# A hybrid decoder step: probabilities times cached values, with the cached rows as the stationary operand in plain float32

## The chip, the cores and the metric

The kernel runs on one core of one Trainium2 chip. The metric is the device time of one execution in microseconds (us). It was run three times before the change: 1616.27 us is the median, 1614.43 and 1624.24 the ends. A profiled execution gives the trace that all rows below come from. PE is the matrix engine (TensorE), PEld its weight loads, DVE the vector engine, ACT the scalar engine, POOL the GpSimd engine, SP the engine that issues the DMAs. The profile gives PE's granted clock as a share of full speed; its two levels are 0.5 (1.2 GHz) and 1.0 (2.4 GHz).

## The reference

One layer of a decoder runs over a prompt of 1024 tokens and over 8 sampled sequences of 8 new tokens. The layer's input projection feeds an attention group (8 heads of 64, three dilated windows whose weights are merged) and a state-space group; their outputs are normalised and go through an output projection and a gated feed-forward network. The change concerns the attention of the sampled tokens alone, which reads 2048 cached rows of K and V for each sequence:

```python
def _branch_sample(q, k_all, v_all, window, dil):
    n = window // dil
    idx = lbuf + jnp.arange(t)[:, None] - dil * jnp.arange(n + 1)[None, :]
    ...
    kg = k_all[:, idx]
    vg = v_all[:, idx].astype(F32)
    scores = jnp.einsum('bthe,btkhe->bhtk', q, kg, preferred_element_type=F32) * (HEAD_DIM ** -0.5)
    ...
    out = jnp.einsum('bhtk,btkhe->bthe', p / den, vg)
```

The change is in how the last line is computed: for each sequence b and head h, the sum over cached rows of a probability (8 new tokens) times a row of V (64 numbers).

## The kernel before, in words

The program is one instruction stream for each engine; a planner sets the order of instructions by the timeline that it reckons, within what the code's generators (`merge`, with paces) hand it. It has these stages: the input projection (`phase_a`, with the sampled tokens' scores, `sample_scores`), then `phase_b`, then the output projection and the feed-forward network (`phase_e`), which takes more than half of the time.

`phase_b` has two halves. In the first, the state-space recurrence (`ssm_main`), the prompt's attention (`prompt_attn`) and the softmax of the first four sampled sequences run side by side. In the second, which this text calls **the value stage**, three streams run side by side: the state-space gate (`ssm_gate`, tiles mixS, w, sg), the values of the sampled tokens (`sample_values`) and the rest of the prompt's attention. Of that attention these names appear in rows: KH, KL and QS are keys and queries (scores, into a bank pmm), P the probabilities, PT their transposes (from a bank ptr), VS the values (into the bank ppo).

The numbers of most products are float32 split in two parts of the type float32r, a rounded "hi" and a remainder "lo" (`split`: an ACT copy that rounds, then a DVE or POOL subtraction), since a float32r product goes through PE in one pass; a plain float32 product appears in the trace as two matmul records with a weight load each.

`sample_values` takes 10 units of 128 cached rows for each of 8 sequences, 80 units in all. For a unit, `vload` (SP, tile vr, six buffers, five units ahead) brings 128 rows of 512 numbers (8 heads of 64). `vsplit` writes vs: hi on ACT, lo on DVE or POOL (POOL for even units). `mult` issues two matmuls: the stationary operand is PX, the probabilities of 8 heads and 8 tokens as 64 columns of hi and 64 of lo, and vs moves past it, 512 columns of hi and then of lo, so every head's probabilities meet every head's values. After the tenth unit, vn (the new rows, 64 partitions) is added with PN. The bank then holds 64 times 512 numbers of which the blocks with equal heads are wanted: `gather1` masks them with hsel and adds over heads on DVE, `gather2` turns them with a matmul by csel and two ACT copies write mixA. `soft1` to `soft3` make the probabilities of the later sequences on the way; `soft3` splits them into PX and PN.

Of the kernel before, what the change touches and what calls it, by code (L numbers as in the profile page):

```python
# [10 lines left out]
F32 = mybir.dt.float32  # L11
F32R = mybir.dt.float32r
I32 = mybir.dt.int32
AF = mybir.ActivationFunctionType
OP = mybir.AluOpType
AX = mybir.AxisListType
# [15 lines left out]
FPOOL, PPOOL, VPOOL, HSP = ((3,), (1, 3, 5), (1, 3, 5), (1, 3, 5)), ((0, 1),), (0, 2, 4, 6, 8), (1, 3, 5, 7)  # L32
XPOOL = (3, 4, 5, 6, 7, 8)
CLAG, CS, X1, LG, VG, LA, TLAG, NLAG = 1, 2, 5, 3, 4, 3, 3, 1
PB, VB, VSB, KKB, PTB, TAB, TCB, HSB, UB, CSB, WSB, HB = 10, 6, 4, 2, 2, 3, 2, 3, 2, 3, 5, 5
# [7 lines left out]
def raw(ap):  # L43
    return ap.bitcast(F32)


class K:
# [701 lines left out]
    def sample_values(self, sp):  # L749
        nc, I = self.nc, self.I  # L750
        V = nc.vector
        S = self.S
        cv = I["cache_attn_v"][0].rearrange("b p h e -> b p (h e)")
        hsel = sp.tile([128, 8], F32, name="hsel")
        sel = sp.tile([128, 68], F32, name="sel")
        csel = sp.tile([128, 64], F32, name="csel")
        self.load(hsel, I["c_hsel"])
        self.load(sel, I["c_sel"])
        self.load(csel, I["c_csel"])
        vn = sp.tile([64, 2, 512], F32R, name="vn")  # L760
        vnr = sp.tile([128, 1152], F32, tag="pv", name="vnr", bufs=1)[:64, 0:512]
        self.load(vnr, self.O[7].rearrange("o b t h e -> (o b t) (h e)"))
        self.split(vn[:, 0], vn[:, 1], vnr)
        PX, PN, mx = {}, {}, {}


        def soft1(g):
            sl = sp.tile([128, 1152], F32, tag="pv", name="sl", bufs=1)[:, 0:NKEY]
            for a in range(2):
                self.load(sl[64 * a:64 * a + 64], I["c_slnc"][2 * g + a].unsqueeze(0).to_broadcast((8, 8, NKEY)))  # L770
            mx[g] = sp.tile([128, 2], F32, tag="mx", name="mx", bufs=2)
            V.tensor_tensor_reduce(out=S[:, g], in0=S[:, g], in1=sl, scale=-1.0, scalar=3e38, op0=OP.add, op1=OP.min, accum_out=mx[g][:, 0:1])
            nc.scalar.activation(S[:, g], S[:, g], AF.Exp, bias=mx[g][:, 0:1], scale=-1.0, accum_out=mx[g][:, 1:2])

        def soft2(g):
            V.reciprocal(mx[g][:, 1:2], mx[g][:, 1:2])
            V.tensor_scalar(S[:, g], S[:, g], mx[g][:, 1:2], None, op0=OP.mult)

        def soft3(g):
            PX[g] = sp.tile([128, 2, 10, 2, 64], F32R, tag="PX", name="PX", bufs=2)
            PN[g] = sp.tile([64, 2, 2, 64], F32R, tag="PN", name="PN", bufs=2)
            Z = sp.tile([128, 1152], F32, tag="pv", name="Z", bufs=1)
            V.tensor_tensor(Z[:, 0:768].rearrange("p (a t) -> p a t", t=8), S[:, g, 0:96].unsqueeze(2).to_broadcast((128, 96, 8)),
                            sel[:, 0:8].unsqueeze(1).to_broadcast((128, 96, 8)), op=OP.mult)
            V.tensor_tensor(Z[:, 768:1152].rearrange("p (a t) -> p a t", t=4), S[:, g, 96:192].unsqueeze(2).to_broadcast((128, 96, 4)),
                            sel[:, 8:12].unsqueeze(1).to_broadcast((128, 96, 4)), op=OP.mult)
            for j0, n in ((0, 4), (4, 4), (8, 2)):
                p = self.bank("sd")  # L790
                for j in range(n):
                    src = Z[:, 128 * (j0 + j):128 * (j0 + j) + 128] if j0 + j < 9 else S[:, g, 192:320]
                    self.tr(p[:, 128 * j:128 * j + 128], src)
                if n == 2:
                    self.tr(p[:64, 256:384], S[:, g, 320:384])
                    self.split(PN[g][:, :, 0], PN[g][:, :, 1], p[:64, 256:384].rearrange("p (b c) -> p b c", b=2))
                for a in range(2):
                    pa = p[:, 0:128 * n].rearrange("p (j b c) -> p b j c", j=n, b=2)[:, a]
                    d = PX[g][:, a, j0:j0 + n]
                    self.split(d[:, :, 0], d[:, :, 1], pa)  # L800


        vr, vs, po, rb = {}, {}, {}, {}
        NU = 10

        def vload(i):
            if i >= 8 * NU:
                return
            b, u = divmod(i, NU)
            vr[i] = self.sv.tile([128, 512], F32, tag="vr", name="vr", bufs=VB)  # L810
            if u < 6:
                self.load(vr[i], cv[b, 256 * u:256 * u + 256].rearrange("(a r) f -> a r f", r=16)[:, 0:8])
            else:
                self.load(vr[i], cv[b, 768 + 128 * u:896 + 128 * u])

        def vsplit(i):
            b, u = divmod(i, NU)
            s = vs[i] = self.sv.tile([128, 2, 512], F32R, tag="vs", name="vs", bufs=VSB)
            nc.scalar.activation(s[:, 0], vr[i], AF.Copy)  # L819
            eng = nc.gpsimd if u in VPOOL else V  # L820
            eng.tensor_tensor(out=s[:, 1], in0=vr[i], in1=raw(s[:, 0]), op=OP.subtract)  # L821

        def mult(i):
            b, u = divmod(i, NU)
            if u == 0:
                po[b] = self.bank("sd")
            p, s = po[b], vs[i]
            x = PX[b // 2][:, b % 2, u].rearrange("p a c -> p (a c)")
            for hl in range(2):
                self.mm1(p, x, s[:, hl], start=(u == 0 and hl == 0), stop=False)  # L830
            if u == NU - 1:
                for hl in range(2):
                    self.mm1(p, PN[b // 2][:, b % 2].rearrange("p a c -> p (a c)"), vn[:, hl], False, hl == 1)

        def gather1(b):
            pv = sp.tile([128, 1152], F32, tag="pv", name="pv", bufs=1)[:, 0:512].rearrange("p (h e) -> p h e", e=64)
            V.tensor_tensor(pv, po[b].rearrange("p (h e) -> p h e", e=64), hsel.unsqueeze(2).to_broadcast((128, 8, 64)), op=OP.mult)
            rb[b] = sp.tile([128, 2, 64], F32, tag="rb", name="rb", bufs=1)
            V.tensor_reduce(rb[b][:, 0], pv.rearrange("p h e -> p e h"), axis=AX.X, op=OP.add)
            V.tensor_copy(rb[b][:, 1], rb[b][:, 0])  # L840

        def gather2(b):
            pa = self.bank("sd")
            self.mm1(pa[:, 0:64], rb[b].rearrange("p a e -> p (a e)"), csel)
            pav = pa[:, 0:64].rearrange("p (f a t) -> p f a t", f=4, a=2)
            cs = slice(1024 + 8 * b, 1032 + 8 * b)
            nc.scalar.activation(self.mixA[0:64, :, cs], pav[0:64, :, 0], AF.Copy)
            nc.scalar.activation(self.mixA[64:128, :, cs], pav[64:128, :, 1], AF.Copy)
        for g in range(2):
            soft1(g)  # L850
            yield 1.0
            soft2(g)
            yield 1.0
            soft3(g)
            yield 1.0
        yield None
        for i in range(VB - 1):
            vload(i)
        for i in range(8 * NU + 3):
            vload(i + VB - 1)  # L860
            if i < 8 * NU:
                vsplit(i)
            if 2 <= i < 8 * NU + 2:
                mult(i - 2)
            b, u = divmod(i, NU)
            if b < 7:

                if b % 2 == 1 and u in (1, 4, 7) and b > 1:
                    (soft1, soft2, soft3)[(1, 4, 7).index(u)](b // 2 + 1)
            if i >= NU + 2 and u == 2:  # L870
                gather1(b - 1)
            if i >= NU + 4 and u == 4:
                gather2(b - 1)
            yield 0.45
        gather2(7)


    def ssm_main(self, sp):
# [1033 lines left out]
def consts():  # L1912
    d = {"c_ident": np.eye(128, dtype=np.float32)}
# [5 lines left out]
    r = np.arange(128)[:, None]  # L1919
# [4 lines left out]
    n, m = np.arange(128)[:, None], np.arange(128)[None, :]  # L1924
# [4 lines left out]
    t = np.arange(8)[:, None]  # L1929
# [4 lines left out]
    for b in range(8):  # L1934
        new[b, :, b, :] = lnc(t - np.arange(8)[None, :])
    d["c_slnc"] = np.concatenate([np.broadcast_to(far, (8, 8, 96)), np.broadcast_to(mid, (8, 8, 96)), np.broadcast_to(near, (8, 8, 128)), new.reshape(8, 8, 64)], axis=2)

    r = np.arange(128)
    d["c_hsel"] = (r[:, None] // 8 % 8 == np.arange(8)[None, :]).astype(np.float32)
    d["c_csel"] = (r[:, None] % 64 == np.arange(64)[None, :]).astype(np.float32)  # L1940

    d["c_sel"] = np.concatenate([r[:, None] % 8 == np.arange(8), r[:, None] % 4 == np.arange(4),
                                 r[:, None] // 8 == np.arange(16), r[:, None] // 4 == np.arange(32), (r[:, None] + 4) % 8 == np.arange(8)], axis=1).astype(np.float32)
# [27 lines left out]
```

## Time and the profile before

| | |
|---|---|
| Median of 3 runs | 1616.27 us |
| Profiled execution | 1614.53 us, of which span 1612.8 us (first to last instruction) |
| Granted clock of PE over the span | 0.923 |
| Busy share of the span: PE, PEld, DVE, ACT, POOL | 91%, 84%, 74%, 45%, 54% |
| The first matmul on vs starts, the last rows on vs | 495.0 us, 659.0 us from the span's start |

A group's mean time of a PE instruction is its latency, and matmuls overlap. What one costs PE is read from the start of one row of the timeline to the start of the next, divided by the number of matmuls in it.

### The profile page before, as it was taken

The page shows a single profiled execution, that of the slowest core. Times are in us where ns is not written, and L with a number is a line of the kernel's source. Part 1 is how long each engine was busy: PE and PEld are TensorE (multiplying, and loading weights), DVE is VectorE, ACT ScalarE, POOL GpSimd, SP SyncE. Part 2 cuts the span into 40 slices and gives each one's busy share as a digit, 9 for nine tenths or more (in the row PEclk, how much of TensorE's full clock was granted, in tenths as well). Part 3 has the DMA queues.
Part 4 walks back from the last instruction along what each step waited for, and adds up shares of the span by engine and source line. Part 5 has one row for each costly group of instructions (what it writes and reads, how often), then busy time and mean ns, then how long its engine had stood idle before and what let it go on. Part 6 is the DMA issues. An engine that isn't in the chain of part 4 may idle for free.

```text
span 1612.8 us, 27931 instructions
## 1 busy us (share of the span) xinstructions
PE 1466.1 (91%) x9909; PEld 1362.1 (84%) x9909; DVE 1193.3 (74%) x2310; ACT 720.3 (45%) x1831; POOL 877.8 (54%) x807
## 2 busy tenths in 40 slices
PE   6988779788899999899887999999999979988896
PEld 5988769776777777689887999999999979978896
DVE  6887589938866787777989555555555598789785
ACT  6232334434456767665443333333333354454343
POOL 3065354407734545545568655555553386578772
PEclk9998879866878999789998999999999999999998
DMA  8445698689746873534322222333332383474654
GB/s 217 149 159 180 202 262 242 197 198 223 203 129 178 214 195 98 157 95 130 96 88 83 91 94 92 99 102 101 102 102 70 109 296 111 149 285 137 187 163 122
DMA packets 212953, 246.20 MB, mean 153 GB/s; under 512 B 26798, under 2 KB 164878, under 8 KB 212814
## 3 DMA queue, kind: packets, MB, share of 16 engines
q1 hardware_dynamic: 212814, 244.43, 51.3%
q8 instruction: 78, 1.28, 0.3%
q14 instruction: 61, 0.50, 0.1%
HBM read 184.43 MB, written 59.95 MB: 152 GB/s over the span
## 4 chain that ended last, share of the span: by engine, by line
PE 62%; DVE 18%; DMA 9%; issue 5%; POOL 3%; ACT 2%; SPq 1%; DVEq 0%; POOLq 0%; ACTq 0%
PE pmm L72 14%; PE pmm L70 14%; PE pmm L71 14%; PE psd L75 7%; PE pmm L75 4%; DVE ws L65 3%; PE ppo L75 3%; PE ptr L79 2%; DMA kk<-in_cache_attn_k_dram 1%; DVE hT L1540 1%; DVE hn L65 1%; DMA kf<-in_cache_attn_k_dram 1%; SPq L82 1%; DMA hs<-dH 1%; PE psd L79 1%
## 5 line engine op out<-in xcount | busy, mean ns | idle before, releaser
L70 PE MATMUL pmm<-hn,ws 128*128 128x272 f32 x1232 | 359.0, 291 | 10.2 <-DVE s L1694 6.4
L72 PE MATMUL pmm<-hn,ws 128*128 128x272 f32 x1232 | 357.2, 291 | 3.4 <-DVE ws L65 3.4
L71 PE MATMUL pmm<-hn,ws 128*128 128x272 f32 x1232 | 357.4, 290 | 2.1 <-DVE hn L65 2.1
L65 DVE TENSOR_TENSOR ws<-wr,ws 128x512 fp32r<-128x512 f32 (+2 forms) x240 | 254.9, 1071 | 32.1 <-ACT ws L64 31.5
L70 PEld LDWEIGHTS pmm<-hn,ws 128*128 128x128 f32 x1232 | 233.9, 190 | 11.1 <-issue 7.7
L71 PEld LDWEIGHTS pmm<-hn,ws 128*128 128x128 f32 x1232 | 234.1, 190 | 2.8 <-DVE hn L65 2.7
L72 PEld LDWEIGHTS pmm<-hn,ws 128*128 128x128 f32 x1232 | 232.9, 189 | 4.0 <-DVE ws L65 3.9
L64 ACT ACTIVATE ws<-wr 128x512 fp32r<-128x512 f32 (+2 forms) x240 | 152.5, 642 | 176.5 <-PE pmm L72 169.1
L65 DVE TENSOR_TENSOR ws<-st,ws 128x512 fp32r<-128x512 f32 (+1 forms) x136 | 132.5, 978 | 81.3 <-ACT ws L64 80.6
L64 ACT ACTIVATE ws<-st 128x512 fp32r<-128x512 f32 (+1 forms) x136 | 83.6, 616 | 135.7 <-PE pmm L72 101.5
L72 PE MATMUL pmm<-hs,ws 128*128 128x272 f32 x448 | 133.6, 299 | 8.5 <-DVE ws L65 7.8
L70 PE MATMUL pmm<-hs,ws 128*128 128x272 f32 x448 | 132.3, 295 | 5.1 <-DVE hid L1694 4.8
L71 PE MATMUL pmm<-hs,ws 128*128 128x272 f32 x448 | 132.0, 295 | 1.3 <-DVE hs L65 1.3
L1614 POOL TENSOR_TENSOR st<-wr 128x512 f32<-128x512 f32 x40 | 56.8, 1419 | 101.7 <-DVE ws L65 101.1
L1701 POOL TENSOR_TENSOR hid<-hid,s 128x272 f32<-128x272 f32 x88 | 82.2, 940 | 43.4 <-DVE hid L1694 43.3
L821 POOL TENSOR_TENSOR vs<-vr,vs 128x512 fp32r<-128x512 f32 x40 | 53.6, 1346 | 90.5 <-ACT vs L819 88.8
L674 POOL TENSOR_TENSOR kf<-kf,qb 128x1024 f32<-128x1024 f32 x24 | 60.1, 2510 | 76.7 <-DMA kf<-in_cache_attn_k_dram 60.5
L1622 POOL TENSOR_TENSOR st<-wr,st 128x512 f32<-128x512 f32 x40 | 57.5, 1437 | 79.5 <-DVE ws L65 79.5
L72 PEld LDWEIGHTS pmm<-hs,ws 128*128 128x128 f32 x448 | 86.1, 193 | 11.4 <-DVE ws L65 11.1
L70 PEld LDWEIGHTS pmm<-hs,ws 128*128 128x128 f32 x448 | 86.2, 192 | 5.7 <-issue 5.0
L1118 DVE CUSTOM_DVE_ANT_0 P<-pmm,lnc 128x256 f32<-128x256 f32 (+1 forms) x128 | 47.9, 377 | 56.7 <-PE pmm L75 39.8
L71 PEld LDWEIGHTS pmm<-hs,ws 128*128 128x128 f32 x448 | 86.3, 193 | 1.5 <-DVE hs L65 1.5
(441 smaller groups left out, 4262.2 us busy)
## 6 DMA issues: line engine op xcount, KB each, us to landing
vr<-in_cache_attn_v_dram SPq DMA_DIRECT2D x80, 256.0 KB
wr<-in_ffn_w_down_dram SPq DMA_DIRECT2D x32, 512.0 KB
hs<-dH SPq DMA_DIRECT2D x28, 544.0 KB
kf<-in_cache_attn_k_dram SPq DMA_DIRECT2D x48, 256.0 KB
wr<-in_ffn_w_gate_dram SPq DMA_DIRECT2D x24, 512.0 KB
wr<-in_ffn_w_up_dram SPq DMA_DIRECT2D x24, 512.0 KB
dH<-hid SPq DMA_DIRECT2D x22, 544.0 KB
wr<-in_w_in_dram SPq DMA_DIRECT2D x16, 512.0 KB
```

The lines of the kernel that those rows point to most:

```text
L64: self.nc.scalar.activation(hi, src, AF.Copy)
L65: (eng or self.nc.vector).tensor_tensor(out=lo, in0=src, in1=raw(hi), op=OP.subtract)
L70: nc.tensor.matmul(out, lhsT=wh, rhs=xh, start=start, stop=False)
L71: nc.tensor.matmul(out, lhsT=wh, rhs=xl, start=False, stop=False)
L72: nc.tensor.matmul(out, lhsT=wl, rhs=xh, start=False, stop=stop)
L75: self.nc.tensor.matmul(out, lhsT=w, rhs=x, start=start, stop=stop)
L79: self.nc.tensor.transpose(out, in_, self.ident[:n, :n])
L674: nc.gpsimd.tensor_tensor(out=kf[i], in0=kf[i], in1=qb[b][:, 0:1].to_broadcast((128, 2, 512)), op=OP.mult)
L821: eng.tensor_tensor(out=s[:, 1], in0=vr[i], in1=raw(s[:, 0]), op=OP.subtract)
L1614: G.tensor_tensor(out=s1, in0=a[:, :, 128:256], in1=b[:, :, 128:256], op=OP.add)
L1622: self.nc.gpsimd.tensor_tensor(out=s2, in0=b[:, :, 0:128], in1=s2, op=OP.subtract)
L1701: G.tensor_tensor(out=o, in0=o, in1=sb, op=OP.mult)
```

## The change

`vsplit`, `gather1` and the mask hsel and matrix csel go. `mult` now takes the loaded rows vr themselves as the stationary operand, in plain float32: four matmuls for a unit, one for each pair of heads (128 columns of vr), with the 16 probabilities of that pair (2 heads of 8 tokens) moving. After the tenth unit four more take vn and PN. The result lies with the 128 numbers of the head pair on partitions, so `place` copies it to mixA with two ACT copies where `gather2` did. vr is now kept until its matmuls are done; the tile vs is gone. `soft3` copies the probabilities with ACT and splits nothing.

```diff
--- before.py
+++ after.py
@@ -751,16 +751,10 @@
         V = nc.vector
         S = self.S
         cv = I["cache_attn_v"][0].rearrange("b p h e -> b p (h e)")
-        hsel = sp.tile([128, 8], F32, name="hsel")
         sel = sp.tile([128, 68], F32, name="sel")
-        csel = sp.tile([128, 64], F32, name="csel")
-        self.load(hsel, I["c_hsel"])
         self.load(sel, I["c_sel"])
-        self.load(csel, I["c_csel"])
-        vn = sp.tile([64, 2, 512], F32R, name="vn")
-        vnr = sp.tile([128, 1152], F32, tag="pv", name="vnr", bufs=1)[:64, 0:512]
-        self.load(vnr, self.O[7].rearrange("o b t h e -> (o b t) (h e)"))
-        self.split(vn[:, 0], vn[:, 1], vnr)
+        vn = sp.tile([64, 512], F32, name="vn")
+        self.load(vn, self.O[7].rearrange("o b t h e -> (o b t) (h e)"))
         PX, PN, mx = {}, {}, {}
 
 
@@ -779,8 +773,8 @@
 
 
         def soft3(g):
-            PX[g] = sp.tile([128, 2, 10, 2, 64], F32R, tag="PX", name="PX", bufs=2)
-            PN[g] = sp.tile([64, 2, 2, 64], F32R, tag="PN", name="PN", bufs=2)
+            PX[g] = sp.tile([128, 10, 2, 64], F32, tag="PX", name="PX", bufs=2)
+            PN[g] = sp.tile([64, 2, 64], F32, tag="PN", name="PN", bufs=2)
             Z = sp.tile([128, 1152], F32, tag="pv", name="Z", bufs=1)
             V.tensor_tensor(Z[:, 0:768].rearrange("p (a t) -> p a t", t=8), S[:, g, 0:96].unsqueeze(2).to_broadcast((128, 96, 8)),
                             sel[:, 0:8].unsqueeze(1).to_broadcast((128, 96, 8)), op=OP.mult)
@@ -793,14 +787,11 @@
                     self.tr(p[:, 128 * j:128 * j + 128], src)
                 if n == 2:
                     self.tr(p[:64, 256:384], S[:, g, 320:384])
-                    self.split(PN[g][:, :, 0], PN[g][:, :, 1], p[:64, 256:384].rearrange("p (b c) -> p b c", b=2))
-                for a in range(2):
-                    pa = p[:, 0:128 * n].rearrange("p (j b c) -> p b j c", j=n, b=2)[:, a]
-                    d = PX[g][:, a, j0:j0 + n]
-                    self.split(d[:, :, 0], d[:, :, 1], pa)
-
-
-        vr, vs, po, rb = {}, {}, {}, {}
+                    nc.scalar.activation(PN[g].rearrange("p b c -> p (b c)"), p[:64, 256:384], AF.Copy)
+                nc.scalar.activation(PX[g][:, j0:j0 + n].rearrange("p j b c -> p (j b c)"), p[:, 0:128 * n], AF.Copy)
+
+
+        vr, po = {}, {}
         NU = 10
 
         def vload(i):
@@ -813,36 +804,19 @@
             else:
                 self.load(vr[i], cv[b, 768 + 128 * u:896 + 128 * u])
 
-        def vsplit(i):
-            b, u = divmod(i, NU)
-            s = vs[i] = self.sv.tile([128, 2, 512], F32R, tag="vs", name="vs", bufs=VSB)
-            nc.scalar.activation(s[:, 0], vr[i], AF.Copy)
-            eng = nc.gpsimd if u in VPOOL else V
-            eng.tensor_tensor(out=s[:, 1], in0=vr[i], in1=raw(s[:, 0]), op=OP.subtract)
 
         def mult(i):
             b, u = divmod(i, NU)
             if u == 0:
                 po[b] = self.bank("sd")
-            p, s = po[b], vs[i]
-            x = PX[b // 2][:, b % 2, u].rearrange("p a c -> p (a c)")
-            for hl in range(2):
-                self.mm1(p, x, s[:, hl], start=(u == 0 and hl == 0), stop=False)
-            if u == NU - 1:
-                for hl in range(2):
-                    self.mm1(p, PN[b // 2][:, b % 2].rearrange("p a c -> p (a c)"), vn[:, hl], False, hl == 1)
-
-        def gather1(b):
-            pv = sp.tile([128, 1152], F32, tag="pv", name="pv", bufs=1)[:, 0:512].rearrange("p (h e) -> p h e", e=64)
-            V.tensor_tensor(pv, po[b].rearrange("p (h e) -> p h e", e=64), hsel.unsqueeze(2).to_broadcast((128, 8, 64)), op=OP.mult)
-            rb[b] = sp.tile([128, 2, 64], F32, tag="rb", name="rb", bufs=1)
-            V.tensor_reduce(rb[b][:, 0], pv.rearrange("p h e -> p e h"), axis=AX.X, op=OP.add)
-            V.tensor_copy(rb[b][:, 1], rb[b][:, 0])
-
-        def gather2(b):
-            pa = self.bank("sd")
-            self.mm1(pa[:, 0:64], rb[b].rearrange("p a e -> p (a e)"), csel)
-            pav = pa[:, 0:64].rearrange("p (f a t) -> p f a t", f=4, a=2)
+            for f in range(4):
+                fs, ps_ = slice(128 * f, 128 * f + 128), slice(16 * f, 16 * f + 16)
+                self.mm1(po[b][:, ps_], vr[i][:, fs], PX[b // 2][:, u, b % 2, ps_], u == 0 and f == 0, False)
+                if u == NU - 1:
+                    self.mm1(po[b][:, ps_], vn[:, fs], PN[b // 2][:, b % 2, ps_], False, f == 3)
+
+        def place(b):
+            pav = po[b][:, 0:64].rearrange("p (f a t) -> p f a t", f=4, a=2)
             cs = slice(1024 + 8 * b, 1032 + 8 * b)
             nc.scalar.activation(self.mixA[0:64, :, cs], pav[0:64, :, 0], AF.Copy)
             nc.scalar.activation(self.mixA[64:128, :, cs], pav[64:128, :, 1], AF.Copy)
@@ -856,23 +830,18 @@
         yield None
         for i in range(VB - 1):
             vload(i)
-        for i in range(8 * NU + 3):
+        for i in range(8 * NU):
             vload(i + VB - 1)
-            if i < 8 * NU:
-                vsplit(i)
-            if 2 <= i < 8 * NU + 2:
-                mult(i - 2)
+            mult(i)
             b, u = divmod(i, NU)
             if b < 7:
 
                 if b % 2 == 1 and u in (1, 4, 7) and b > 1:
                     (soft1, soft2, soft3)[(1, 4, 7).index(u)](b // 2 + 1)
-            if i >= NU + 2 and u == 2:
-                gather1(b - 1)
-            if i >= NU + 4 and u == 4:
-                gather2(b - 1)
+            if u == 1 and b:
+                place(b - 1)
             yield 0.45
-        gather2(7)
+        place(7)
 
 
     def ssm_main(self, sp):
@@ -1934,10 +1903,7 @@
     for b in range(8):
         new[b, :, b, :] = lnc(t - np.arange(8)[None, :])
     d["c_slnc"] = np.concatenate([np.broadcast_to(far, (8, 8, 96)), np.broadcast_to(mid, (8, 8, 96)), np.broadcast_to(near, (8, 8, 128)), new.reshape(8, 8, 64)], axis=2)
-
     r = np.arange(128)
-    d["c_hsel"] = (r[:, None] // 8 % 8 == np.arange(8)[None, :]).astype(np.float32)
-    d["c_csel"] = (r[:, None] % 64 == np.arange(64)[None, :]).astype(np.float32)
 
     d["c_sel"] = np.concatenate([r[:, None] % 8 == np.arange(8), r[:, None] % 4 == np.arange(4),
                                  r[:, None] // 8 == np.arange(16), r[:, None] // 4 == np.arange(32), (r[:, None] + 4) % 8 == np.arange(8)], axis=1).astype(np.float32)
```

The two listings that follow show PE in the second half of the value stage, around the last of the twelve products of `ssm_gate` (mixS); names are those of the section above, out<-in, then the output's partitions and columns. Before:

```order
L75 MATMUL psd<-vs,PX 128x512 x8
L75 MATMUL psd<-csel,rb 128x64
L75 MATMUL psd<-vs,PX 128x512
L75 MATMUL pmm<-KH,QS 128x128
L75 MATMUL pmm<-KL,QS 128x128
L75 MATMUL psd<-vs,PX 128x512 x3
L75 MATMUL psd<-mixS,w 128x320 x4
L75 MATMUL psd<-vs,PX 128x512
```

Now:

```order
L75 MATMUL ppo<-PT,VS 128x128 x2
L79 MATMUL ptr<-ident,P 128x128 x3
L75 MATMUL psd<-PX,vr 128x16 x12
L75 MATMUL pmm<-KH,QS 128x256 x2
L75 MATMUL pmm<-KL,QS 128x256 x2
L75 MATMUL ppo<-PT,VS 128x256
L79 MATMUL ptr<-ident,P 128x128 x4
L75 MATMUL ppo<-PT,VS 128x256
L75 MATMUL ppo<-PT,VS 128x128 x4
L75 MATMUL psd<-PX,vr 128x16 x4
L75 MATMUL psd<-mixS,w 128x320 x4
```

The runs of 512-column matmuls became runs of 16-column ones, each a plain float32 product; the matmuls of the two other streams stay between them.

On ACT, where the softmax of the last two sampled sequences starts (S, mx) in the value stage, this stood before (sg is the gate's output, e and ST belong to the prompt's softmax):

```order
L819 ACTIVATE vs<-vr 128x512 x2
L1128 ACTIVATE P,ST<-P,ST 128x256
L819 ACTIVATE vs<-vr 128x512 x2
L64 ACTIVATE PX<-psd 128x2x64
L1128 ACTIVATE P,ST<-P,ST 128x128
L819 ACTIVATE vs<-vr 128x512
L773 ACTIVATE S,mx<-S,mx 128x384
L1128 ACTIVATE P,ST<-P,ST 128x128
L1032 ACTIVATE sg<-psd,gb 128x384
```

Now, at the same place:

```order
L821 ACTIVATE mixA<-psd 64x4x8
L822 ACTIVATE mixA<-psd 64x4x8
L767 ACTIVATE S,mx<-S,mx 128x384
L64 ACTIVATE PT<-ptr 128x512
L1097 ACTIVATE P,ST<-P,ST 128x128
L1125 ACTIVATE e<-e 128x32
L1097 ACTIVATE P,ST<-P,ST 128x128
L1204 ACTIVATE tmp<-ppo 64x512
L1061 ACTIVATE VS<-VR 128x8x64 x2
L1001 ACTIVATE sg<-psd,gb 128x384
```

The ACT copies of vr are gone from between the attention's own instructions, and nothing stands in their place.

## Rows read from the trace of the kernel before

**Rows 1.** The page: granted clock in 40 slices, and the chain that ended last.
```profile
PEclk9998879866878999789998999999999999999998
...
PE 62%; DVE 18%; DMA 9%; issue 5%; POOL 3%; ACT 2%; SPq 1%; DVEq 0%; POOLq 0%; ACTq 0%
```

**Rows 2.** Busy time by stretch: us, PE, PEld, DVE, ACT, POOL, granted clock, DMA, GB/s.
```profile
340.00:400.00 60.00, 51.61 (x195) 39.56 (x195) 41.24 (x134) 26.59 (x91) 30.83 (x50) 0.61 0.97 231
400.00:450.00 50.00, 43.12 (x225) 36.33 (x224) 39.75 (x113) 23.09 (x71) 36.92 (x57) 0.81 0.74 187
450.00:495.00 45.00, 44.19 (x199) 35.80 (x199) 28.67 (x93) 31.47 (x81) 13.78 (x23) 0.73 0.67 161
495.00:675.00 180.00, 176.46 (x841) 130.90 (x839) 139.30 (x335) 124.74 (x320) 95.45 (x122) 0.95 0.58 157
```

**Rows 3.** Costliest groups, 495 to 675 us: busy, mean ns, idle before and releaser.
```profile
L75 PE MATMUL psd<-vs,PX 128*128 128x512 f32 x160 | 56.3, 462 | 0.3 <-POOL vs L821 0.3
L821 POOL TENSOR_TENSOR vs<-vr,vs 128x512 fp32r<-128x512 f32 x39 | 52.4, 1347 | 76.7 <-ACT vs L819 75.1 <-DMA vr<-in_cache_attn_v_dram 1.5
L819 ACT ACTIVATE vs<-vr 128x512 fp32r<-128x512 f32 x76 | 44.9, 622 | 9.4 <-PE psd L75 8.1 <-DMA vr<-in_cache_attn_v_dram 0.5 <-ACT vs L819 0.4
...
L821 DVE TENSOR_TENSOR vs<-vr,vs 128x512 fp32r<-128x512 f32 x39 | 33.0, 849 | 3.1 <-ACT vs L819 2.8 <-ACT PT L64 0.2
```

**Rows 4.** SP's waits, 495 to 675 us: total, times, longest.
```profile
SPq L82 <- POOL vs L821: 36.1, 22, 4.7
...
SPq L82 <- DVE vs L821: 19.7, 12, 6.7
```

**Rows 5.** PE's timeline in the value stage: start, length, instruction, count.
```profile
576.39 0.73 PE L75 MATMUL psd<-vn,PN 64*128 64x512 f32 x2
577.05 0.39 PE L75 MATMUL pmm<-KH,QS 128*128 128x256 f32 x1
577.37 0.38 PE L75 MATMUL pmm<-KL,QS 64*128 64x256 f32 x1
...
582.53 3.76 PE L75 MATMUL psd<-vs,PX 128*128 128x512 f32 x8
586.09 0.31 PE L75 MATMUL pmm<-KH,QS 128*128 128x128 f32 x1
...
627.96 2.12 PE L75 MATMUL psd<-vs,PX 128*128 128x512 f32 x8
629.91 0.33 PE L75 MATMUL psd<-csel,rb 128*128 128x64 f32 x2
```

**Rows 6.** PE's timeline where plain float32 with 16 columns moves already.
```profile
97.25 0.96 PE L75 MATMUL psd<-E,vt 128*128 128x16 f32 x8
98.07 0.43 PE L71 MATMUL pmm<-xT,ws 128*128 128x384 f32 x1
...
358.72 0.60 PE L75 MATMUL pmm<-KH,QS 128*128 128x256 f32 x1
359.25 0.60 PE L75 MATMUL pmm<-KL,QS 64*128 64x256 f32 x1
359.78 2.74 PE L75 MATMUL psd<-sel,Z 128*128 128x16 f32 x12
362.36 2.75 PE L75 MATMUL psd<-sel,Y 128*128 128x32 f32 x12
```

**Rows 7.** Busy time by stretch, around three places, columns as in Rows 2.
```profile
361.70:365.10 3.40, 3.40 (x17) 3.40 (x18) 2.25 (x5) 0.08 (x1) 0.00 (x0) 0.50 1.11 215
365.10:371.90 6.80, 6.56 (x21) 4.88 (x20) 5.34 (x15) 3.52 (x11) 2.09 (x3) 0.50 1.14 247
...
576.70:580.10 3.40, 3.40 (x21) 2.58 (x19) 2.63 (x7) 2.27 (x7) 1.28 (x1) 1.00 1.03 219
580.10:583.50 3.40, 3.40 (x13) 2.79 (x13) 2.62 (x9) 2.12 (x6) 0.00 (x0) 0.50 1.03 237
...
586.90:590.30 3.40, 3.40 (x13) 2.42 (x14) 2.63 (x8) 2.10 (x7) 1.90 (x2) 0.99 0.40 86
```

## The prediction

> **What bounds the kernel now.** I read the page first: the clock in 40 slices is lowest in slices 9 and 10 (323 to 403 us), and the chain of work that ended last lies on PE for 62% of the span [rows 1]. So the question is what the change does to PE, and at which clock. Then the busy times by stretch [rows 2]: in the value stage, 495 to 675 us, PE is busy for 176.5 of 180 us, DVE for 139, ACT for 125, POOL for 95. A busy PE need not be a full one, so I looked at the idle times as well: before its largest group there, the 160 matmuls on vs, PE waited 0.3 us in all [rows 3]. The splits on ACT, DVE and POOL keep ahead of it, and POOL waits 76.7 us for its turn [rows 3]. PE bounds this stage, and the three other engines have slack in it. The reader should see as well that the two stretches ahead of it, which hold the same prompt attention beside small float32 products but no 512-column matmuls, ran at a granted clock of 0.61 and 0.81, and the value stage at 0.95 [rows 2].
>
> **What is removed.** From ACT 80 copies of 622 ns, from DVE 40 subtractions of 849 ns, from POOL 40 of 1347 ns [rows 3], and the mask-and-add of the results on DVE. None of it holds up PE (0.3 us), so it gives back nothing, except the few waits that a wide margin removes. From PE it takes the 160 matmuls on vs: eight in a row cost 629.91 - 627.96 = 1.95 us at the full clock, 0.244 us each, and 586.09 - 582.53 = 3.56 us at the half clock, 0.445 us each [rows 5]. The 16 matmuls on vn cost (577.05 - 576.39) / 2 = 0.33 us each [rows 5]. At the full clock that is 160 x 0.244 + 16 x 0.33 = 44 us. The 16 small records on csel are left in the rest below; they are worth about 1 us.
>
> **What is added.** 80 units and 8 groups on vn make 88 groups of four plain float32 matmuls, 128 x 128 stationary and 16 columns moving. The trace has exactly that form: four matmuls on E and vt, eight records, take 98.07 - 97.25 = 0.82 us at the full clock [rows 6], 0.103 us a record. At the half clock the twelve records on sel and Z take 362.36 - 359.78 = 2.58 us [rows 6], 0.215 us a record, so 1.72 us a group. What is paid there is the weight loads: in 361.7 to 365.1 us PEld is busy for all of the 3.4 us [rows 7]. So one unit costs PE 0.82 us where it cost 0.49 us, or 1.72 us where it cost 0.89 us. In all: 88 x 0.82 = 72 us at the full clock against 44, and 88 x 1.72 = 151 us at the half clock. The groups on vn load weights of 64 partitions between ones of 128, which the rows show for KH and KL alone. Its price lies between nothing and the difference of a vn and a vs record, 0.09 us, on 128 records: 0 to 11 us. I take 0, since the eight-record row is the nearest in form, and keep the other end for the range.
>
> **Loads and queues.** The same 80 loads of vr stand in SP's queue, but a buffer now comes free after the matmuls and not after the subtraction. SP waited 36.1 us for POOL's and 19.7 us for DVE's subtractions of vs [rows 4]; those waits pass to PE. Behind a waiting load stand the loads of the next head's KH, KL and QS, and the scores wait for those. Five units stay ahead; at 311 / 80 = 3.9 us a unit (below) that is 19 us, against a longest wait of 6.7 us now, and the DMA engines are busy for 0.58 of the stage [rows 2]. I count nothing. The softmax tail now has copies in place of splits and is off PE's path: nothing. The listing starts the stage with seven score pairs of the prompt more inside it than before. That moves work from one stage to the next; at 0.53 us a matmul (KH and KL at the half clock, 359.25 - 358.72 [rows 6]) it is 7 us that the first half of the phase gives and the value stage takes, and I leave both out.
>
> **The clock, which decides.** With the full clock the sum would be small. Three places in the rows say that it does not stay. First, at 359.78 us PE runs 24 small float32 records on end at 0.50; in 361.7 to 365.1 us PE and PEld are busy without a gap, and still the next 6.8 us are at 0.50 [rows 6, 7]. Second, in 576.7 to 580.1 us PE is busy without a gap at 1.00 with products of 64 partitions, outputs of 128 columns and transposes, and the next stretch falls to 0.50 [rows 7]. Third, from there eight matmuls on vs, of 512 columns, run back to back at the half clock (582.53), and from 586.9 us the clock is 0.99 [rows 5, 7]. So in this kernel the clock does not follow how busy PE is; the long matmuls lift it and short ones behind weight loads do not. The change removes the 512-column matmuls from the very stage whose clock they hold at 0.95, and puts 16-column ones there, in runs of up to twelve.
>
> **The sum.** A clock of 0.95 means a tenth of the 180 us at the half clock. With half-clock work 1.75 times as long (0.445 / 0.244 = 1.8 for vs; 0.53 against 577.37 - 577.05 = 0.32, so 1.7, for KH [rows 5, 6]) the stage is 162 + 18 / 1.75 = 172 us of full-clock work, and what is left without values is 172 - 44 = 128 us, its small stalls with it. The new stage is then 128 + 72 = 200 us wholly at the full clock and 128 x 1.7 + 151 = 369 us wholly at the half clock. With a share h of its time at the half clock it is 200 / (1 - 0.458 h) us. For h I take the stretch 340 to 400 us, at 0.61, so h = 0.78: of the four stretches it is the nearest in kind, since there the prompt's scores stand among runs of small float32 products with nothing of 512 columns. The one at 0.81 has h = 0.38; it is PE-busy for 43 of 50 us and less crowded with small float32 runs. h = 0.78 gives 200 / 0.643 = 311 us, which is 131 us more than 180. Against the profiled execution's 1614.53 us that is **1745 us**; that execution lies 1.7 us below the median of the runs, so the change is about 8%.
>
> **Rivals.** (1) The clock stays as it is, h = 0.1: 200 / 0.954 = 210 us, 30 us more, 1644 us, slower by under 2%. For it: mixS products of up to 384 columns remain in the stage, and E and vt ran at the full clock at 97 us [rows 6], between long matmuls. Against it: the first two places above. The Trainium skill, page "TensorE: Matmul & The Clock Gate", section "Why this matters for your kernels", tells to keep TensorE busy without long idle gaps, and the full rate then holds. By that rule this rival is what happens, since PE hardly idles; this trace disagrees at 361.7 and at 576.7 us, where PE was busy for 3.40 of 3.40 us and the clock was 0.50 in the stretch that followed [rows 7].
> (2) The new matmuls cost less than the old, because their weights are loaded behind the neighbours' matmuls. It decides if a record adds under some 0.04 us; at 0.03 us the 704 records are 21 us, the stage 149 / 0.954 = 156 us, and the time 1591 us, faster by 1.5%. For it: between two KH and KL matmuls lie 0.32 us, in which a load would fit. Against it: the runs of eight and twelve in rows 6 hide nothing, at 0.103 us a record, and the new order has runs like those. The Trainium skill, same page, section "Back-to-back issue gap", gives about 25 ns for a matmul of up to 64 columns by itself. By that figure 704 records would take 18 us, an estimate from the page; the row with 0.103 us a record does not agree, since each record there brings its own weights.
> (3) Between the two: loads half hidden, the clock as now, and the time within 1% of before.
>
> **How the numbers follow.** That the clock is low for a third of the stage or more (h from 0.35 to 1: 1673 to 1804 us) has a chance of 0.78; the likeliest is 1745. Rival 1, with h below 0.35, 1634 to 1673 us, has 0.12; rival 2 has 0.04, rival 3 has 0.04, and 0.02 is left for more than 1804 us. One per cent, 16 us, is about what a measurement of this kernel can tell from no change. Faster by over 1%: 0.04; within 1%: 0.04; slower by over 1%: 0.92. The range takes in the forecast's own span down to its low end and cuts a little at the top, since h = 1 would need the mixS products to lift nothing: 1670 to 1798 us.
>
> **What would show it.** In the profile after: a value stage of about 310 us; a granted clock of about 0.6 in it (1 - 0.78 / 2); eight records on vr and PX from start to start about 0.8 us where the clock is 1.00 and 1.7 us where it is 0.50; PE still busy for nearly all of the stage, and ACT, DVE and POOL far from it; no long wait on loads of vr. Rival 1 would show the same rows with a clock of 0.9 or more and a stage of 210 us; rival 2 records on vr some 0.03 us apart. The forecast is wrong if the clock recovers on the mixS and score matmuls often enough, or if another engine or SP's loads set the pace and PE idles.

## The result and the profile after

The changed kernel takes 1752.88 us (median of 4 runs, 1744.92 to 1756.36) where the kernel before took 1615.35 us beside it: a ratio of 1.0829, with a 95% interval of 1.0778 to 1.088. (The ratios here are estimated from all runs; the quotient of these two medians is 1.085.) It is slower by 8%. Its profiled execution took 1756.36 us, of which the span is 1754.6 us, at a granted clock of 0.857 over the whole.

The page of the kernel after, the same two lines as [rows 1]:

```profile
PEclk9988889858765666555999799999999998999999
...
PE 64%; DVE 17%; DMA 8%; issue 4%; SPq 2%; POOL 2%; ACT 2%; DVEq 0%; POOLq 0%; ACTq 0%
```

A slice is 44 us here. Slices 12 to 19 (483 to 833 us) hold the value stage and read 5 to 6; the kernel before had 7 to 9 in the slices of its value stage, 13 to 17 of 40 us each [rows 1]. Behind the stage both rows stay at 8 to 9, but for one slice after.

Busy time by stretch, kernel after, columns as in [rows 2]; the stage begins 6 us earlier (first matmul on vr at 488.69 us, on vs at 495.0 us) and ends at 816.5 us, where the next stage's first product stands, which was at 673.4 us:

```profile
340.00:400.00 60.00, 39.45 (x153) 31.83 (x152) 31.24 (x96) 18.59 (x63) 21.80 (x36) 0.57 0.86 194
400.00:450.00 50.00, 45.97 (x250) 38.05 (x249) 40.27 (x127) 27.03 (x89) 36.10 (x64) 0.89 0.87 209
450.00:489.00 39.00, 37.29 (x169) 30.49 (x169) 26.12 (x87) 24.60 (x58) 17.00 (x29) 0.68 0.65 174
489.00:817.00 328.00, 327.60 (x1396) 281.50 (x1395) 87.80 (x272) 92.85 (x258) 39.68 (x83) 0.59 0.34 92
```

The value stage is 328 us where it was 178. PE is busy for 327.6 of them, ACT and DVE for less than a third, and the clock is 0.59 where [rows 2] had 0.95. So nothing holds PE up; PE itself is slow. The whole difference of the two profiled executions is there: 1756.36 - 1614.53 = 141.8 us, of which the stage is +149.4, what lies ahead of it -6.3 and what lies behind it -1.3.

Groups of the value stage after, columns as in [rows 3], and the largest of SP's waits, as in [rows 4]:

```profile
L75 PE MATMUL psd<-PX,vr 128*128 128x16 f32 x640 | 131.2, 336 | 0.0
...
L75 PE MATMUL psd<-mixS,w 128*128 128x384 f32 x64 | 38.5, 752 | 0.0
```

```profile
SPq L82 <- PE psd L75: 235.2, 78, 8.0
```

SP now waits for PE before nearly every load of vr, 235.2 us in all. It costs nothing, since five units stay ahead and the groups on vr and mixS had no idle time before them (the last column is 0.0).

PE's timeline after, columns as in [rows 5]: one run of vr at each clock, and the place where vr and vn take turns:

```profile
506.01 1.01 PE L75 MATMUL psd<-PX,vr 128*128 128x16 f32 x8
506.88 0.36 PE L75 MATMUL pmm<-KH,QS 128*128 128x256 f32 x1
...
527.86 0.61 PE L75 MATMUL psd<-PX,vr 128*128 128x16 f32 x2
528.39 0.61 PE L75 MATMUL psd<-PN,vn 64*128 64x16 f32 x2
528.93 0.61 PE L75 MATMUL psd<-PX,vr 128*128 128x16 f32 x2
...
584.86 3.43 PE L75 MATMUL psd<-PX,vr 128*128 128x16 f32 x16
588.13 0.56 PE L75 MATMUL pmm<-KH,QS 128*128 128x256 f32 x1
```

At the full clock a unit of eight records takes 506.88 - 506.01 = 0.87 us, 0.109 us a record; at the half clock sixteen take 588.13 - 584.86 = 3.27 us, 0.204 us a record, so 1.64 us a unit. Where vr and vn take turns, two records take 0.53 us, 0.27 us each.

### The profile page after: what moved, and what is told of

It is laid out like the page before. It is cut to its first block, busy times and chain, and to the rows that moved or that the text cites. A ratio compares the mean times of both kernels' runs of the same rounds, so it can differ in the third digit from the quotient of the medians.

```text
span 1754.6 us, 28590 instructions
## 1 busy us (share of the span) xinstructions
PE 1603.2 (91%) x10421; PEld 1504.1 (86%) x10421; DVE 1127.0 (64%) x2217; ACT 677.8 (39%) x1738; POOL 819.0 (47%) x767
## 4 chain that ended last, share of the span: by engine, by line
PE 64%; DVE 17%; DMA 8%; issue 4%; SPq 2%; POOL 2%; ACT 2%; DVEq 0%; POOLq 0%; ACTq 0%
PE pmm L72 13%; PE pmm L70 13%; PE pmm L71 13%; PE psd L75 12%; PE pmm L75 4%; PE ppo L75 4%; DVE ws L65 4%; PE ptr L79 3%; SPq L82 2%; DVE hT L1509 1%; DVE hn L65 1%; DMA kf<-in_cache_attn_k_dram 1%; DMA kk<-in_cache_attn_k_dram 1%; DVE hs L65 1%; DMA QS<-dQ 1%
## 5 line engine op out<-in xcount | busy, mean ns | idle before, releaser
L1140 POOL TENSOR_SCALAR P<-P,f 128x256 f32<-128x256 f32 (+1 forms) x118 | 53.6, 483 | 238.5 <-DVE f L1129 165.6
L75 PEld LDWEIGHTS psd<-PX,vr 128*128 128x128 f32 x640 | 131.0, 295 | 7.1 <-issue 4.3
L75 PE MATMUL psd<-PX,vr 128*128 128x16 f32 x640 | 131.2, 336 | 0.0
L1097 ACT ACTIVATE P<-P,ST 128x256 f32<-128x256 f32 (+1 forms) x128 | 60.1, 470 | 101.5 <-DVE ST L1087 100.0
L72 PEld LDWEIGHTS pmm<-hs,ws 128*128 128x128 f32 x448 | 87.1, 195 | 11.2 <-DVE ws L65 10.3
```

Of the source, the lines that this page charges most:

```text
L72: nc.tensor.matmul(out, lhsT=wl, rhs=xh, start=False, stop=stop)
L75: self.nc.tensor.matmul(out, lhsT=w, rhs=x, start=start, stop=stop)
L1097: nc.scalar.activation(x, x, AF.Exp, bias=st[:, 0], scale=-1.0, accum_out=st[:, 1])
L1140: G.tensor_scalar(x, x, fc, 1.0, op0=OP.mult, op1=OP.mult)
```

## The experiments

Two theories stood after this. **The clock theory:** most of the loss is the low clock, which the runs of short plain float32 products bring because the 512-column products that lifted it are gone. **The price theory:** what is dear is the product itself, with its two records and two weight loads, and the clock is a small part or a bystander. Each experiment but the sixth edits the kernel after; the ratio is always to the kernel before. The kernel before had medians of 1613.10 us beside the first three, 1614.20 us beside the next three and 1615.26 us beside the last two.

**1. Plain float32, but with the old roles.** The probabilities stand (64 columns) and vr moves, 512 columns; mask and turn come back. One thing is kept from the change, the plain float32 product, and with it the 512-column products return.

```diff
-            for f in range(4):
-                fs, ps_ = slice(128 * f, 128 * f + 128), slice(16 * f, 16 * f + 16)
-                self.mm1(po[b][:, ps_], vr[i][:, fs], PX[b // 2][:, u, b % 2, ps_], u == 0 and f == 0, False)
...
+            self.mm1(po[b][:64], PX[b // 2][:, u, b % 2], vr[i], u == 0, False)
+            if u == NU - 1:
+                self.mm1(po[b][:64], PN[b // 2][:, b % 2], vn, False, True)
```

> The changed kernel with the roles of the plain float32 product swapped back: the probabilities of 8 heads stand (64 columns), the 512 numbers of the cached rows move, and the mask and the turn of the results return. No splits, same loads. A unit is two records of 512 columns; from the 384-column float32 records of the gate (about 0.3 us each at the full clock) I estimate 0.8 to 0.85 us a unit, the price of the change's eight short records (0.82). Clock theory: long matmuls hold the clock at 0.9 or more, the stage lasts 200 to 215 us, the whole 1635 to 1655 us. Rival (the price of plain float32 products on PE is what the change pays, and the clock would fall anyway): as the change, 1740 to 1760 us, clock in the stage near 0.6.

Measured: 1659.56 us (1655.44 to 1666.73), ratio 1.0292 (1.0217 to 1.0368). The value stage of this kernel by stretch, and one run of four units in PE's timeline:

```profile
489.00:717.00 228.00, 223.49 (x859) 124.27 (x860) 100.05 (x297) 92.00 (x254) 38.10 (x83) 0.96 0.48 131
```

```profile
567.52 3.65 PE L75 MATMUL psd<-vr,PX 128*64 128x512 f32 x8
571.10 0.48 PE L75 MATMUL pmm<-KH,QS 128*128 128x128 f32 x1
```

A unit is two records here, and four units take 571.10 - 567.52 = 3.58 us: 0.895 us a unit, at the full clock, a little more than the 0.87 us of the kernel after. Yet the stage is 228 us and not 328, at a clock of 0.96 and not 0.59. The dearer product at the higher clock loses 3%, the cheaper one at the lower clock 8%. The rival's 1740 to 1760 us are far off; the clock theory's own ranges (200 to 215 us, 1635 to 1655 us) were a little low, in part since a unit was expected to cost 0.8 to 0.85 us.

**2. Long products put back as ballast.** After each of a sequence's first nine units four float32r matmuls of zeros, 448 columns, into columns of the bank that nobody reads: 288 in all, pure extra work.

```diff
+            if u < NU - 1:
+                for _ in range(4):
+                    self.mm1(po[b][:, 64:512], zr[:, 0:128], zr[:, 64:512], False, False)
```

> The changed kernel with four further float32r matmuls of 448 columns after each of the first nine units of a sequence (288 in all), zeros times zeros, added into columns of the unit's bank that nobody reads. They are pure extra work on PE: some 0.2 us each at the full clock, 0.39 us at the half, so 58 to 112 us. Clock theory: they lift the clock in the stage to 0.8 to 0.9, which pays for them; the stage stays between 285 and 340 us and the whole between 1710 and 1770 us. Rival (the records themselves cost the time, not the clock): the extra work adds up, 1810 to 1865 us.

Measured: 1768.51 us (1763.23 to 1775.4), ratio 1.0955 (1.0884 to 1.1025). The stage by stretch, and the added group:

```profile
480.00:825.00 345.00, 345.00 (x1661) 298.79 (x1661) 87.74 (x268) 90.45 (x251) 36.93 (x83) 0.75 0.32 87
```

```profile
L75 PE MATMUL psd<-zr 128*128 128x448 f32 x288 | 102.4, 480 | 0.0
```

PE was busy for 102 us with work that nobody needs, and the kernel took 16 us more than the kernel after. The rest was paid by the clock, which rose from 0.59 to 0.75. That fits the clock theory in kind, and the rival's 1810 us or more did not come. But the clock rose less than the 0.8 to 0.9 expected, and the stage is longer than the 340 us given as its upper end, so ballast doesn't win here. Whether ballast of other numbers than zeros would have raised the clock further was not tried.

**3. Few of the new products.** The matmuls on vr of only the first and the tenth unit of each sequence are issued, with those on vn; the values of the other eight units are left out of the result. Loads and all else stay.

```diff
-                self.mm1(po[b][:, ps_], vr[i][:, fs], PX[b // 2][:, u, b % 2, ps_], u == 0 and f == 0, False)
+                if u in (0, NU - 1):
+                    self.mm1(po[b][:, ps_], vr[i][:, fs], PX[b // 2][:, u, b % 2, ps_], u == 0 and f == 0, False)
```

> The changed kernel with the value matmuls of only the first and the tenth unit of each sequence (it leaves out 8 of 10 units; all loads stay): 64 of 80 groups of eight short records go, 52 us of PE at the full clock, 110 us at the half. Clock theory: what is left has no 512-column matmuls either, so the clock stays well under the 0.95 of the kernel before (0.7 to 0.85), the stage is 170 to 200 us, the whole 1600 to 1630 us. Rival (the short records alone pull the clock down): the rest runs at 0.95, the stage is about 155 us, the whole about 1585 us. Rival (records cost their half-clock time, the rest does not change): 326 - 110 = 216 us, about 1643 us.

Measured: 1642.51 us (1641.5 to 1646.39), ratio 1.0176 (1.0115 to 1.0238). The stage by stretch:

```profile
484.00:702.00 218.00, 213.67 (x877) 169.15 (x877) 86.78 (x272) 92.50 (x257) 38.43 (x83) 0.68 0.50 139
```

The time lies beyond what the clock theory gave and beside the price theory's number, so this run by itself speaks against the clock theory as it was put, and a part of that falls. If the short products pulled the clock down, it should have come back for the most part with 24 of 88 groups left; it came back to 0.68 alone. But the price theory doesn't explain the stage either: a stage that does less work than the one before the change (by the forecast's terms 128 + 24 x 0.82 = 148 us of full-clock work against 172) takes 218 us and not 178, with PE idle for 4 us of it. The trace of this run has a place that tells more. Its last record on vn starts at 664.80 us; from 665.4 us on the stage holds the prompt's attention alone:

```profile
665.40:684.00 18.60, 18.60 (x74) 15.92 (x73) 7.40 (x22) 10.58 (x26) 3.00 (x4) 0.50 0.00 1
694.50:702.00 7.50, 6.22 (x52) 5.54 (x50) 4.14 (x6) 2.98 (x5) 1.07 (x4) 1.00 0.01 3
```

For 18.6 us PE was busy without a gap and without a value product, and the clock stayed at 0.50; later, behind a wait of PE, the same kind of work ran at 1.00. So the attention runs at either clock and doesn't always raise it by itself, even with the short products gone. That what is missing in this stage are the 160 long products is the likeliest reading beside the runs above and below; this run doesn't show it alone.

**4 and 5. The same instructions with more columns moving.** Blocks, weights, number of records and loads stay; 128 or 64 columns of probabilities move instead of 16, of which the other 112 or 48 belong to other heads and sequences and are not read. The two ACT copies at the end of a sequence become eight smaller ones.

```diff
-                self.mm1(po[b][:, ps_], vr[i][:, fs], PX[b // 2][:, u, b % 2, ps_], u == 0 and f == 0, False)
+                self.mm1(po[b][:, fs], vr[i][:, fs], PX[b // 2][:, u].rearrange("p b c -> p (b c)"), u == 0 and f == 0, False)
```

> The changed kernel with the same stationary blocks, the same number of matmuls and of weight loads, but all 128 probability columns of the pair of sequences move past each block, of which 16 are used; eight small copies place a sequence's result where two did. Only the columns grow, eightfold; 128 columns in plain float32 take about as long as the weight load that each record pays anyway (0.11 us). Clock theory: the stage is back at a clock of 0.9 or more, lasts 205 to 230 us, the whole 1635 to 1665 us, so useless columns make the kernel 90 to 120 us faster. Rival (the time is in the records and their weight loads): no gain, 1745 to 1765 us.

> As the run with 128 columns, but the 64 columns of the own sequence move. Clock theory: between the change and the 128 columns, clock 0.75 to 0.9 in the stage, which lasts 240 to 280 us; the whole 1660 to 1710 us. Rival (records and loads): 1745 to 1765 us.

Measured with 128 columns: 1657.79 us (1652.04 to 1664.19), ratio 1.0265 (1.0225 to 1.0305). With 64: 1703.41 us (1701.17 to 1708.98), ratio 1.0555 (1.0529 to 1.0582). Their stages by stretch, 128 columns first:

```profile
483.00:721.00 238.00, 236.45 (x1393) 196.96 (x1394) 86.91 (x272) 101.16 (x306) 39.37 (x83) 0.93 0.48 127
```

```profile
484.00:764.00 280.00, 279.94 (x1392) 238.33 (x1393) 87.57 (x272) 100.65 (x306) 39.30 (x83) 0.74 0.40 108
```

Read the number of PE's instructions first: 1393 and 1392 records here, 1396 in the kernel after. PE's instructions are the same but for their columns, every value product moves eight or four times as many, and the stage falls from 328 to 238 and 280 us as its clock goes from 0.59 to 0.93 and 0.74. Two unbroken rows of records in the trace with 128 columns give the price of one:

```profile
516.50 2.72 PE L75 MATMUL psd<-PX,vr 128*128 128x128 f32 x22
518.98 0.57 PE L75 MATMUL pmm<-KH,QS 128*128 128x256 f32 x1
...
574.13 3.59 PE L75 MATMUL psd<-PX,vr 128*128 128x128 f32 x16
577.56 1.46 PE L75 MATMUL psd<-mixS,w 128*128 128x384 f32 x4
```

It is (518.98 - 516.50) / 22 = 0.113 us at the full clock and (577.56 - 574.13) / 16 = 0.214 us at the half (granted 0.52 there), against 0.109 and 0.204 us with 16 columns: a little dearer at either clock. So no price of a record explains the gain; what changed is how much of the stage ran at which clock. These are the clearest runs for the clock theory: 1752.88 - 1657.79 = 95 us of the change's 138 are the clock. Both whole times lie in the clock theory's ranges; the stage with 128 columns is 8 us longer than its range, and the clock with 64 is just under its 0.75.

**6. The kernel before with half of its long products.** Only the hi part of V is made and multiplied for the cached rows; the remainder's contribution to the values is left out.

```diff
-            for hl in range(2):
-                self.mm1(p, x, s[:, hl], start=(u == 0 and hl == 0), stop=False)
+            self.mm1(p, x, s[:, 0], start=(u == 0), stop=False)
```

> The kernel before, without the remainder of V (it leaves out the lo part of vs, so the sampled tokens' values are less exact): one 512-column float32r matmul a unit in place of two, no subtraction on DVE or POOL. 80 x 0.244 = 20 us of PE at the full clock go. If half of the long matmuls still hold the clock at 0.88 or more, the stage gives back 12 to 20 us and the whole is 1592 to 1603 us. If the clock falls with them to 0.75 or less, nothing is gained: 1612 us or more.

Measured: 1607.24 us (1598.75 to 1610.14), ratio 0.9949 (0.9922 to 0.9975). The stage by stretch:

```profile
493.00:668.00 175.00, 167.84 (x747) 124.68 (x746) 100.26 (x295) 122.88 (x317) 41.51 (x83) 0.86 0.60 162
```

Eighty matmuls at 0.244 us [rows 5] are 20 us of PE's work less, and the stage is 3 us shorter; 7 us came back in all (1614.20 - 1607.24). That lies between the two outcomes expected (1592 to 1603 us, or 1612 and more). Of the missing 17 us some 4 are idle time of PE (175 - 167.84 = 7.2 us, where the kernel before had 180 - 176.46 = 3.5 [rows 2]); the rest fits the clock, 0.86 where it was 0.95 (by the forecast's kind of sum 172 - 20 = 152 us of full-clock work make 174 us at 0.86). The long products partly pay for themselves in the kernel before, too.

**7 and 8. vn apart from vr.** In the kernel after, and in that of experiment 4, the matmuls on vn of a sequence's tenth unit are issued together behind its four on vr, where the two took turns. The matmuls are the same.

```diff
-                if u == NU - 1:
+            if u == NU - 1:
+                for f in range(4):
+                    fs, ps_ = slice(128 * f, 128 * f + 128), slice(16 * f, 16 * f + 16)
                     self.mm1(po[b][:, ps_], vn[:, fs], PN[b // 2][:, b % 2, ps_], False, f == 3)
```

> The kernel after, with the matmuls on vn of a sequence's tenth unit issued together behind its four on vr, where the two took turns; the same matmuls in all. Theory A: taking turns between weights of 64 and of 128 partitions costs. In the changed kernel two records took 0.53 us at the half clock there (527.86, 528.39, 528.93) against 2 x 0.205 in runs of vr alone, 0.06 us more each, so 128 records are worth up to 8 us: 1743 to 1749 us, with rows of eight vr records and of eight vn records about 1.64 us long. Theory B: the extra time is that of any short pair at this place, and grouping gives nothing: 1750 to 1758 us.

> The kernel with 128 moving columns, of which 16 are used, with the same grouping of the matmuls on vn, at a clock near full. There two records that take turns took 0.42 us (565.41, 565.83, 566.25) against 2 x 0.115 in runs, 0.095 us more each: by theory A 128 records are worth up to 12 us, so 1645 to 1651 us against the 1658 us of the kernel with 128 columns. By theory B it stays at 1655 to 1661 us.

Measured with 16 columns: 1735.28 us (1732.18 to 1745.06), ratio 1.0757 (1.0729 to 1.0785). With 128: 1641.43 us (1638.22 to 1643.75), ratio 1.0162 (1.0143 to 1.0182). Both gain more than either theory gave them: on the kernel after 17.6 us by the medians and 12 us by the ratios, whose two intervals just touch, so its size is uncertain; on experiment 4 16.4 us by the medians and 17 by the ratios. The stage of the kernel after (first row below) and of experiment 7 (second fence), each up to the point where 1352 of PE's records are done, and the vn run of experiment 7:

```profile
489.00:810.00 321.00, 321.00 (x1352) 275.04 (x1352) 86.42 (x270) 91.00 (x253) 39.68 (x83) 0.59 0.35 94
```

```profile
487.00:788.00 301.00, 301.00 (x1352) 256.78 (x1353) 86.52 (x270) 91.24 (x254) 39.59 (x83) 0.63 0.37 100
```

```profile
560.08 1.72 PE L75 MATMUL psd<-PN,vn 64*128 64x16 f32 x8
561.73 1.65 PE L75 MATMUL psd<-mixS,w 128*128 128x384 f32 x2
```

In a run a vn record takes (561.73 - 560.08) / 8 = 0.206 us at the half clock, as one on vr does; in turns it was 0.27. So taking turns costs 0.06 us a record, 8 us over 128 records if all stand at the half clock. Two things change with the turns: weights of 64 and of 128 partitions follow each other, and four records in a row, where runs have two, add into the same 16 columns of the bank. No run separates them. But the prompt's attention has runs with four in a row into the same columns and weights of 128 partitions alone, as here in experiment 2, where the clock was 0.50:

```profile
821.71 3.65 PE L75 MATMUL ppo<-PT,VS 128*128 128x128 f32 x16
825.16 1.01 PE L75 MATMUL ptr<-ones,acc 128*68 128x1 f32 x8
```

They take 3.45 / 16 = 0.216 us each, about what a record with 128 columns takes in experiment 4, so the change of partitions is the likelier of the two. What was gained beyond 8 us goes with a clock of 0.63 against 0.59. Why grouping should raise it was not tried. Experiment 8 does the same with 128 columns; its stage up to 707 us ran at 0.98, where experiment 4 had 0.93:

```profile
486.00:707.00 221.00, 219.17 (x1400) 185.23 (x1399) 87.51 (x273) 101.05 (x308) 40.09 (x83) 0.98 0.51 137
```

Neither of the two, nor any other version that computes the whole result, is faster than the kernel before.

## Why the prediction was right

The forecast was 1745 us, within a range of 1670 to 1798; 1752.88 us came. Point by point:

**What bounds the stage.** It was PE, and is: 327.6 of 328 us busy, no idle time before the new groups. The removed splits, copies and masks could give nothing back, as was said: PE had hardly waited for them [rows 3]. SP's waits passed to PE, as was said, and cost nothing.

**The price of the new product.** Forecast 0.82 us a unit at the full clock and 1.72 at the half, measured 0.87 and 1.64. The nearest rows in form, E and vt [rows 6], had it right to 6%.

**The groups on vn.** This is the term that was mis-sized. The bounds were 0 to 11 us and 0 was taken. The direct cost is 8 us at the half clock; with the clock that comes along it is 12 us by the ratios and 17.6 us by the medians, beyond the upper end. The reason given, the nearest row in form, was not good enough: the row had the form of one record and not the turns from one kind to the other. The row of vn itself, 0.09 us above one of vs [rows 5], was the one to go by.

**The moved score pairs.** They were said to take some 7 us from what lies ahead of the stage and to bring it into the stage. What lies ahead is 6.3 us shorter, and the stage holds 47 products of 256 columns on KL where it held 40. That the forecast left both sides out nearly cancels in the whole, and not in the stage.

**The clock.** h = 0.78 was taken from the stretch at 0.61; the stage ran at 0.59, so h = 0.82. The full-clock work follows as 328 x (1 - 0.458 x 0.82) = 205 us, where the forecast had 200. With 205 and h = 0.78 the stage would be 319 us, with h = 0.82 it is 328: half of the 17 us above the forecast's 311 is the work (vn, 0.87 for 0.82, the moved score pairs), half the clock. The 6.3 us ahead of the stage took back a part of it. The same sum, with each run's own clock, gives the other stages as well (estimates): 205 + 58 us of ballast at 0.75 make 341 us, measured 345; the 148 us of experiment 3 at 0.68 make 209 us, measured 218 with 4 us idle. So work and clock together account for the time, and neither alone does.

The choice of h carried the size. With the other stretch that the prediction weighed, at 0.81 and h = 0.38, its sum gives 242 us and 1677 us. That the nearer stretch came within 0.02 of the clock is better than one row can promise: the same stretches of the kernel after, whose work the change did not touch but for the moved scores, read 0.57 and 0.89 where they had read 0.61 and 0.81. There was luck in it.

**The reason for the clock.** The prediction had two parts: that long products lift it, and that short ones behind weight loads do not. Experiments 4 and 5 show the first (more columns in the same records, a higher clock and a shorter stage), experiment 3 corrects the weight of the second: most of the short ones can be gone, and the clock is still low. It isn't the 512 columns as such: experiment 8 has no product of 512 columns in its stage, which ran at 0.98, above the 0.95 of the kernel before. What in the products the clock answers to, beyond that more moving columns went with more of it, stays open.

**The rivals.** Rival 1, the clock stays, would have had 0.9 or more in the stage and 1644 us. Experiment 8, with the clock at 0.98 up to 707 us, takes 1641.43 us: the rival's sum was about right and its condition did not hold. Rival 1 is what would have come by the rule of the Trainium skill, page "TensorE: Matmul & The Clock Gate", section "Why this matters for your kernels", that a TensorE kept busy without long gaps keeps the full rate. The trace after disagrees, with PE busy for 327.6 of 328 us at 0.59. Rival 2, weight loads hidden behind neighbours, would have had records 0.03 us apart; they are 0.109 us apart at the full clock. Rival 3 fell with it.

**Where the 138 us are.** From before to experiment 8: 26 us, the price of plain float32 products at about the old clock (with their useless columns). From there to experiment 7, the same with 16 columns: 94 us, the clock (fewer columns cost no more). From there to the kernel after: 18 us (12 by the ratios), vr and vn in turns, some of it clock again. Together 1752.88 - 1615.35 = 137.5.

## What to carry to other kernels

Where PE bounds a stage, cost a new matmul at both clocks, and look in the trace for a stretch that already runs on such matmuls, to see which clock it was granted: that one row decided the size here, and PE's busy share told nothing. Where two such stretches read differently, as here 0.61 and 0.81, keep both in the range. A long product taken out may have been what held the clock for everything around it; here half of the long products taken out gave back 3 us of 20 in their stage. Where a new sequence of instructions changes kind from one to the next, price it by a row that does the same, not by a row of one kind.

## What was not expected of the hardware

More useless columns made the program faster: 16, 64 and 128 moving columns in the same 704 records gave stages of 328, 280 and 238 us at clocks of 0.59, 0.74 and 0.93. A stage with only a few of the value products (experiment 3) ran at 0.68 with PE busy for 213.67 of 218 us, and 18.6 us of attention alone in it at 0.50 with no gap. And weights of 64 and 128 partitions in turns cost 0.27 us a record where each in a run of its own costs 0.205 us at the half clock.
